# First feed-forward half step in two phases: products of half size upward, then downward in groups of four tiles

## The chip, the cores and the metric

The kernel runs on one core of one Trainium2 chip. The metric is the device time of one execution in microseconds (us), from several runs of each kernel. Engines are named as in the profile: PE is TensorE (matmuls; PEld its weight loads), DVE VectorE, ACT ScalarE, POOL GpSimd, and SP the queue that issues most transfers.

## The reference

One layer over 512 latent and 256 context tokens of width 1024: a SwiGLU half step on both streams, a two-part recurrent mixer, a second half step on the latent tokens, a last norm. All is float32. What the change touches is the first half step:

```python
def swiglu(h, w1, w2):
    g, u = jnp.split(h @ w1, 2, axis=-1)
    return (jax.nn.silu(g) * u) @ w2

def ffn_sub(s, mods, nw, w1, w2):
    shift, scale, gate = mods
    return s + 0.5 * gate * swiglu(modulate(rmsnorm(s, nw), shift, scale), w1, w2)

x = ffn_sub(x, mod_lat[0:3], norm1_w[l], ffn1_w1[l], ffn1_w2[l])          # 512 tokens
s_ctx = ffn_sub(s_ctx, mod_ctx[0:3], norm1_w[l], ffn1_w1[l], ffn1_w2[l])  # 256 tokens
...
x = x + mod_lat[5] * lat_mix
x = ffn_sub(x, mod_lat[6:9], norm3_w[l], ffn2_w1[l], ffn2_w2[l])
return rmsnorm(x, final_norm_w)
```

`w1` is 1024 x 5632 (gate and up halves of 2816 columns each), `w2` 2816 x 1024.

## The kernel before

Activations lie transposed: 128 rows of the width on the partitions, tokens along the free dimension, so that x is 8 tiles (index k or m) of 768 columns, 256 of the context first (`CTX`), then 512 latent ones (`LAT`). Each float32 matrix product is three matmuls on operands split into a high and a low part (`split`, line 78: ACT writes the high part, DVE the low part; `gemm3`, line 248: high x high, high x low, low x high).

The half step runs over 22 tile pairs j of 128 columns, a gate and an up tile each. For each pair, `up` (line 402) makes 8 x 3 matmuls of 512 columns and 8 x 3 of 256 for the gate tile, and as many for the up tile; `act` applies silu and the product and splits the result. After every two pairs, `down` (line 439) multiplies their results with `w2` for each of the 8 tiles of x: 6 matmuls of 512 columns and 6 of 256, and a DVE instruction that adds the PSUM bank times the gate to x. Up and down alternate in PE's program order. The last pair is computed by segments (`up_last`), and its down step runs over three segments of 256 columns while the next norm begins.

The second half step (latent tokens only) already computes most of its pairs another way (`up_fast`, line 306, `ups_fast`, line 375): the pair's 2 x 2 blocks (gate/up by token half, two halves of the width) come from seven block products of half the size (Winograd's form of Strassen's scheme), with sums of weight blocks (S1 to S4, on DVE) and of activation blocks (T1 to T4, made once by `fast_operands`). A product is 4 x 3 matmuls of 256 columns there. It works in steps that are woven between units: `b` is a PSUM bank that takes product after product, and ACT copies it out between them.

Beside this, `hook` (in `_build`, line 1037 on) computes the adaLN modulation for later stages: each of 56 tiles is a 512 KB load and one or two dot products on DVE (`mod_tile`, line 215). In the start phase `more` and its helpers prepare the norm of tile k while PE works on k-1.

Each engine runs its instructions in its own program order. Within `ordered` stretches that is the order written; elsewhere a scheduler fixes it at build time, and semaphores carry the waits. SP issues the loads in order too, and waits there for the buffer that a load fills.

Of the kernel before, what the change touches and what calls it, by code (L numbers as in the profile page):

```python
# [12 lines left out]
P = 128  # L13
# [55 lines left out]

class Builder:  # L70
# [12 lines left out]

    def sq_add(self, S, k, x, n, lanes="vpvpvpvl"):

        nc = self.nc
        lane = lanes[k]
        if n > 512:
            sq = self.fp.tile([P, n], F32, name="ah" if lane in S else "al", bufs=3)
# [125 lines left out]
    def mod_tile(self, i, k):  # L215
        nc = self.nc
        wm = self.modp.tile([P, DM], F32, name="wm", bufs=3)
# [39 lines left out]
    def ffn(self, w1, w2, with_ctx, gate_l, gate_c, hook, first, ahead, then, final=None, more=None, fast=None):  # L257
        nc = self.nc
        G = 2
        off = 0 if with_ctx else NC_  # L260
        AT = NT - off
        segs = [LAT, CTX] if with_ctx else [LAT]

        def load(j):
            ws, banks = self.ffn_load(w1, j)
            return ws, banks + ([self.ps.tile([P, 512], F32, name="mm")] if with_ctx else [])
# [8 lines left out]
        def mm(part, half, k, joint=False):  # L275
# [3 lines left out]
            if with_ctx:  # L279
                st, en = ((k == 0 and half == 0), (k == KT - 1 and half == 1)) if joint else (None, None)  # L280
                self.gemm3(pss[2][:, half * 256:half * 256 + 256], h, l, self.xh[k][:, :NC_], self.xl[k][:, :NC_],
                           k, KT, st, en)

        def act_tiles(j):
            return load2(j), [self.fp.tile([P, AT], dt, name=n, bufs=bufs)
                              for n, dt, bufs in (("sg", F32, 2), ("ah", F32R, 3), ("al", F32R, 3))]

        def gated(part, tiles, lo, n):

            psg, psu = part[1][:2]  # L290
            g, u = ((psg[:, lo - NC_:lo - NC_ + n], psu[:, lo - NC_:lo - NC_ + n]) if lo >= NC_ else
                    (part[1][2][:, :256], part[1][2][:, 256:]))
            sg = tiles[0][:, lo - off:lo - off + n]
            nc.scalar.activation(sg, g, AF.Silu)
            nc.vector.tensor_tensor(out=sg, in0=u, in1=sg, op=ALU.mult)

        def act(part, j):
            w2, tiles = act_tiles(j)
            for lo, n in segs:
                gated(part, tiles, lo, n)  # L300
            sg, ah, al = tiles
            self.split(ah, al, sg)
            self.split(*w2)
            return w2[0], w2[1], tiles[1], tiles[2]

        def up_fast(j):

            H = DM // 2
            half = lambda w: (w[:, :H], w[:, H:])
            pair = lambda: (self.wp.tile([P, DM], F32R, name="whi"), self.wp.tile([P, DM], F32R, name="wlo"))
            u, g = (self.wp.tile([P, DM], F32, name="wraw", bufs=2) for _ in range(2))
            for i, raw in ((0, g), (1, u)):
                nc.sync.dma_start(out=raw, in_=w1[j, i])
            s21, s34 = (fast["s"][:, 2 * (j % 2) + i, :] for i in range(2))
            (S2, S1), (S3, S4), (A11, A12), (A21, A22) = half(s21), half(s34), half(u), half(g)
            self.tt(S1, A21, A22, ALU.add)
            self.tt(S2, S1, A11, ALU.add)  # L320
            self.tt(S3, A11, A21, ALU.add)
            self.tt(S4, S2, A12, ALU.add)
            wa = pair()
            self.split(*wa, u)
            wd = [self.fp.tile([P, H], F32R, name="wd" + x, bufs=2) for x in "hl"]
            self.split(*wd, A22)
            yield
            ws = pair()
            self.split(*ws, s21)
            yield  # L330
            b, a = (self.ps.tile([P, 512], F32, name="mm")[:, :256] for _ in range(2))

            def product(bank, w, at, x, start, stop):
                for q in range(4):
                    ks = slice(at + q * P, at + (q + 1) * P)
                    xh, xl = x(q)
                    for i, (l, r) in enumerate(((w[0], xh), (w[0], xl), (w[1], xh))):
                        nc.tensor.matmul(bank, lhsT=l[:, ks], rhs=r, start=(start and q == 0 and i == 0),
                                         stop=(stop and q == 3 and i == 2), skip_group_check=True)

            block = lambda k0, seg: lambda q: tuple(t[k0 + q][:, seg[0]:seg[0] + seg[1]] for t in (self.xh, self.xl))
            T1, T2, T3, T4 = fast["t"]
            ev = self.fp.tile([P, 3, 256], F32, name="ev", bufs=2)
            p1, u2, u3 = (ev[:, i, :] for i in range(3))
            product(b, wa, 0, block(0, LAT_A), True, True)
            nc.scalar.copy(out=p1, in_=b)
            product(a, wa, H, block(4, LAT_A), True, True)
            self.tt(p1, a, p1, ALU.add)
            yield
            wr = pair()  # L350
            self.split(*wr, s34)
            yield
            product(b, ws, 0, T2, False, True)
            nc.scalar.copy(out=u2, in_=b)
            yield
            c = self.ps.tile([P, 512], F32, name="mm")[:, :256]
            product(c, ws, H, T1, True, True)
            yield
            product(b, wr, 0, T3, False, True)
            nc.scalar.copy(out=u3, in_=b)  # L360
            w2, (sg, ah, al) = act_tiles(j)
            self.tt(sg[:, 256:], c, u3, ALU.add)
            self.split(*w2)
            yield
            product(b, wd, 0, T4, False, True)
            nc.scalar.activation(sg[:, :256], b, AF.Silu, scale=-1.0)
            nc.scalar.activation(sg[:, 256:], sg[:, 256:], AF.Silu, scale=-1.0)
            product(c, wr, H, block(4, LAT_B), False, True)
            self.tt(u2, c, u2, ALU.add)
            both = sg.rearrange("p (h t) -> p h t", h=2)  # L370
            self.tt(both, ev[:, 0:2, :], both, ALU.mult)
            self.split(ah, al, sg)
            yield w2[0], w2[1], ah, al

        def ups_fast(js, turn, done):


            nxt, old = up_fast(js[0]), None
            next(nxt), next(nxt)
            for j in js:  # L380
                cur, nxt = nxt, up_fast(j + 1) if j != js[-1] else None
                next(cur)
                turn()
                if old:
                    done(next(old))
                next(cur)
                if nxt:
                    next(nxt)
                next(cur)
                turn()  # L390
                next(cur)
                if nxt:
                    next(nxt)
                turn()
                next(cur)
                turn()
                old = cur
            turn()
            turn()
            done(next(old))  # L400

        def up(j):
            part = load(j)
# [5 lines left out]
        def up_last(j):  # L409

            part = load(j)
            w2, tiles = act_tiles(j)
            self.split(*w2)
            banks = part[1]
            for lo, n in ((LAT, CTX) if with_ctx else (LAT_A, LAT_B)):
                self.mm_seg([(*part[0][half], banks[half] if lo >= NC_ else banks[2],
                              lo - NC_ if lo >= NC_ else half * 256) for half in range(2)], (lo, n))
                gated(part, tiles, lo, n)
                sg, ah, al = (t[:, lo - off:lo - off + n] for t in tiles)
                self.split(ah, al, sg)  # L420
            return w2[0], w2[1], tiles[1], tiles[2]

        def up_first(js):

            ps = []
            for q, ws in enumerate(first):
                bank = lambda pool, name: pool.tile([P, 512], F32, name=name)
                ps.append((ws, [bank(self.ps, "mm"), bank(self.ps, "mm"),
# [996 lines left out]
```

## Time and profile before

| | before |
|---|---|
| runs | 1355.25, 1349.97, 1352.85 us; median 1352.85 us |
| profiled execution | 1351.87 us, span 1350.1 us |
| busy in the span | PE 1326.4 us (98%), PEld 1183.7 (88%), DVE 943.2 (70%), ACT 512.1 (38%), POOL 39.6 (3%) |
| start, norm and first two pairs | 0 to 75 us |
| first half step, steady | 111 to 587 us |
| mixer and its output projection | about 612 to 1020 us |
| second half step | about 1020 us to the end |

The span is the time between the first and the last instruction of the profile; 1.77 us of the execution lie around it. "Busy" is a union of modelled durations, and matmuls overlap in the pipeline: a matmul of 512 columns is listed with 0.39 us although the next one starts 0.23 us later. What PE needs is therefore read from starts, not from durations.

### The profile page before, as it was taken

The numbers are of one execution on the slowest core, as the hardware profiler recorded it, in microseconds if no ns is written. First come the engines' busy times: TensorE is split into PE (matmuls) and PEld (weight loads), VectorE is DVE, ScalarE is ACT, GpSimd is POOL, SyncE is SP. The second block draws the span as 40 slices with busy tenths as digits, with TensorE's granted clock in tenths as the row PEclk, the third lists the DMA queues.
The fourth block names the chain that finished last, engine by engine and source line by source line (L and its number), as shares of the span: only waits on it lengthen the run. The fifth ranks groups of instructions, "written<-read, shape, count | busy, mean of one in ns | idle before, by whom it ended". The sixth has DMA issues, their size and how long they took to land.

```text
span 1350.1 us, 20599 instructions
## 1 busy us (share of the span) xinstructions
PE 1326.4 (98%) x8426; PEld 1183.7 (88%) x8426; DVE 943.2 (70%) x1540; ACT 512.1 (38%) x894; POOL 39.6 (3%) x51
## 2 busy tenths in 40 slices
PE   8999999999999999999989999999999999999997
PEld 4788888888888888899988788888998999999996
DVE  6988767645645644477497777896668878888765
ACT  5541112112112112176464443444554444444434
POOL 1100000000000000021100000000000000000001
PEclk8999999999999999999999999999999999999998
DMA  7654444234334321022132111113324322223301
GB/s 291 227 175 156 141 140 157 94 125 156 109 110 156 114 90 47 32 81 94 47 106 84 47 32 48 47 64 109 126 94 165 102 94 94 94 94 110 110 17 63
DMA packets 43235, 143.17 MB, mean 106 GB/s; under 512 B 4722, under 2 KB 9202, under 8 KB 43140
## 3 DMA queue, kind: packets, MB, share of 16 engines
q1 hardware_dynamic: 43140, 141.85, 31.2%
q8 instruction: 66, 1.08, 0.3%
q14 instruction: 29, 0.24, 0.1%
HBM read 137.60 MB, written 4.24 MB: 105 GB/s over the span
## 4 chain that ended last, share of the span: by engine, by line
PE 92%; DVE 4%; issue 2%; DMA 1%; ACT 1%; POOLq 0%; POOL 0%; DVEq 0%
PE mm L56 64%; PE aux L56 29%; DVE mod_scr L56 1%; DVE wlo L56 1%; DMA wraw<-in_wo 1%; ACT whi L56 0%; DMA wraw<-in_f1w 0%; DVE x L56 0%; DVE rms_acc L56 0%; DVE s L56 0%; DVE xl L56 0%; DVE w2lo L56 0%; DVE a L56 0%; ACT xh L56 0%; DMA w2lo<-in_cc 0%
## 5 line engine op out<-in xcount | busy, mean ns | idle before, releaser
L56 PE MATMUL mm<-xh,whi 128*128 128x256 f32 (+1 forms) x1460 | 477.4, 328 | 1.2 <-ACT xh L56 1.2
L56 PE MATMUL mm<-xh,wlo 128*128 128x256 f32 (+1 forms) x1460 | 472.8, 325 | 0.8 <-DVE wlo L56 0.8
L56 PE MATMUL mm<-xl,whi 128*128 128x512 f32 (+1 forms) x1392 | 457.1, 329 | 2.8 <-DVE xl L56 2.8
L56 PEld LDWEIGHTS mm<-xh,whi 128*128 128x128 f32 x1460 | 277.4, 190 | 28.1 <-issue 1.8
L56 PEld LDWEIGHTS mm<-xh,wlo 128*128 128x128 f32 x1460 | 276.8, 190 | 24.1 <-DVE wlo L56 1.0
L56 PEld LDWEIGHTS mm<-xl,whi 128*128 128x128 f32 x1392 | 264.7, 190 | 26.3 <-DVE xl L56 4.1
L56 ACT ACTIVATE whi<-wraw 128x1024 fp32r<-128x1024 f32 x100 | 105.6, 1059 | 184.4 <-issue 99.1
L56 DVE TENSOR_TENSOR wlo<-wraw,whi 128x1024 fp32r<-128x1024 f32 x100 | 121.8, 1221 | 73.4 <-ACT whi L56 73.3
L56 PE MATMUL aux<-ah,w2hi 128*128 128x512 f32 (+1 forms) x480 | 171.6, 358 | 0.1
L56 PE MATMUL aux<-al,w2hi 128*128 128x512 f32 (+1 forms) x480 | 170.7, 356 | 0.0
L56 PE MATMUL aux<-ah,w2lo 128*128 128x512 f32 (+1 forms) x480 | 169.9, 354 | 0.0
L56 DVE SCALAR_TENSOR_TENSOR x<-aux,mod_l,x 128x512 f32<-128x512 f32 x160 | 117.7, 746 | 27.7 <-PE aux L56 27.3
L56 DVE CUSTOM_DVE_ANT_0 mod_scr<-wm,cb 128x1024 bf16<-128x1024 f32 x96 | 118.8, 1238 | 9.1 <-DMA wm<-in_w_mod 7.3
L56 PEld LDWEIGHTS aux<-ah,w2lo 128*128 128x128 f32 x480 | 90.8, 189 | 12.9
L56 PEld LDWEIGHTS aux<-ah,w2hi 128*128 128x128 f32 x480 | 91.0, 190 | 11.7 <-ACT ah L56 0.6
L56 PEld LDWEIGHTS aux<-al,w2hi 128*128 128x128 f32 x480 | 91.1, 190 | 10.1
L56 ACT ACTIVATE w2hi<-w2raw 128x1024 fp32r<-128x1024 f32 x44 | 44.6, 1050 | 138.4 <-PE aux L56 135.3
L56 DVE TENSOR_TENSOR sg<-mm,sg 128x512 f32<-128x512 f32 (+1 forms) x49 | 27.2, 562 | 87.8 <-PE mm L56 69.9
L56 ACT ACTIVATE sg<-mm 128x256 f32<-128x256 f32 (+1 forms) x66 | 30.1, 458 | 132.4 <-PE mm L56 132.4
L56 PE MATMUL mm<-tl,whi 128*128 128x256 f32 x204 | 57.7, 283 | 0.0
L56 DVE TENSOR_TENSOR w2lo<-w2raw,w2hi 128x1024 fp32r<-128x1024 f32 x44 | 53.7, 1220 | 1.8 <-ACT w2hi L56 0.6
L56 DVE TENSOR_TENSOR wlo<-s,whi 128x1024 fp32r<-128x1024 f32 x34 | 41.6, 1224 | 17.7 <-ACT whi L56 17.7
(295 smaller groups left out, 1956.6 us busy)
## 6 DMA issues: line engine op xcount, KB each, us to landing
wm<-in_w_mod SPq DMA_DIRECT2D x64, 512.0 KB, 4.7
wraw<-in_f2w SPq DMA_DIRECT2D x44, 512.0 KB, 3.3
wraw<-in_f1w SPq DMA_DIRECT2D x42, 512.0 KB, 3.3
wraw<-in_wi SPq DMA_DIRECT2D x32, 512.0 KB, 3.3
w2raw<-in_f1w SPq DMA_DIRECT2D x24, 512.0 KB, 3.3
w2raw<-in_f2w SPq DMA_DIRECT2D x22, 512.0 KB, 4.3
wraw<-in_wo SPq DMA_DIRECT2D x8, 512.0 KB, 5.4
x<-in_xT SPq DMA_DIRECT2D x8, 384.0 KB, 4.9
```

Of the source, the lines that this page charges most:

```text
L56: r = f(*a, **kw)
```

## The change

The first half step becomes a function of its own, `ffn1`, in two phases. Its first four pairs stay as they were in the up direction (the first two in the start phase). The other 18 pairs (j = 4 to 21) are computed by seven products of half size, as in the second half step, on halves of 384 of the 768 columns: 7 x 12 matmuls of 384 columns. No down step runs between them. Each pair's result (128 x 768) is written to device memory by a POOL transfer (`keep`). Then the down phase runs over five groups of four pairs, and a last one of two: each group's results are loaded again and split, and for each of the 8 tiles of x there are 12 matmuls of 512 and 12 of 256 columns and one addition to x for each segment. `w2` is laid out anew, so that one load serves two tiles of x and four pairs. The modulation tiles are spread over both phases, one per unit and one per tile of x.

x is normalised in place in the start phase, its buffer serves as scratch in the up phase, and x is loaded a second time (POOL, 8 transfers) before the down phase. Buffers of the stage come from a class with three shared names (`six`, `four`, `two`). The second half step and the mixer keep their instruction order on PE, DVE and ACT; in the second half step one copy goes to another tile.

```diff
+class Space1:
+    def tile(self, shape, dt, name=None, bufs=None):
+        return self.pool.tile(shape, dt, name="six", bufs=8)
+    quad = lambda self, dt: self.pool.tile([P, DM], dt, name="four", bufs=5)
+    pair = lambda self: self.pool.tile([P, DM], F32R, name="two", bufs=2)
+    wide = lambda self: self.b.modp.tile([P, NT], F32, name="wm", bufs=2)
+    sums = lambda self, j: [self.quad(F32) for _ in range(2)]
...
+    def up_half(self, w1, j, W, c0, T, space):
+        for i, raw in ((0, g), (1, u)):
+            nc.sync.dma_start(out=raw, in_=w1[j, i])
+        s21, s34 = space.sums(j)
+        (S2, S1), (S3, S4), (A11, A12), (A21, A22) = half(s21), half(s34), half(u), half(g)
+        self.tt(S1, A21, A22, ALU.add)
...
+        wa = pair()
+        self.split(*wa, u)
+        wd = space.last()
+        self.split(*wd, A22)
+        yield
+        ws = pair()
+        self.split(*ws, s21)
+        yield
+        b, a = bank(), bank()
...
+        product(b, wa, 0, block(0, c0), True, True)
+        nc.scalar.copy(out=p1, in_=b)
+        product(a, wa, H, block(4, c0), True, True)
+        self.tt(p1, a, p1, ALU.add)
+        yield
+        wr = pair()
+        self.split(*wr, s34)
+        yield
+        product(b, ws, 0, T2, False, True)
+        nc.scalar.copy(out=u2, in_=b)
+        yield
+        c = bank()
+        product(c, ws, H, T1, True, True)
+        yield
+        product(b, wr, 0, T3, False, True)
...
+        nc.scalar.copy(out=g2, in_=b)
+        self.tt(g2, c, g2, ALU.add)
+        yield
+        product(b, wd, 0, T4, False, True)
+        nc.scalar.activation(g1, b, AF.Silu, scale=-1.0)
+        nc.scalar.activation(g2, g2, AF.Silu, scale=-1.0)
+        product(c, wr, H, block(4, c0 + W), False, True)
+        self.tt(u2, c, u2, ALU.add)
+        both = sg.rearrange("p (h t) -> p h t", h=2)
+        self.tt(both, up_, both, ALU.mult)
+        yield sg
...
+    def ffn1(self, space, first, more, hook, mods, ahead, then):
+        hs = [self.dram.tile([P, NT], F32, name=f"h{j}") for j in range(NJ)]
+        keep = lambda j, sg: nc.gpsimd.dma_start(out=hs[j], in_=sg)
...
+        ops = self.half_operands(space.x, 384, space.operands())
+        unit = lambda j: self.up_half(w1, j, 384, 0, space.T, space)
...
+        self.ups_half(range(4, NJ), unit, nxt, turn, keep)
+        for m in range(KT):
+            nc.gpsimd.dma_start(out=space.x[:, m, :], in_=T["xT"][m])
...
+        for g in range(5):
+            for m in range(KT):
+                if m % 2 == 0:
+                    load_w2(*((g, m // 2 + 1) if m < 6 else (g + 1, 0)))
+                wh, wl = w2[g, m // 2]
+                for seg, gate in ((LAT, self.mod_l), (CTX, self.mod_c)):
+                    lo, n = seg
+                    pb = bank(self.ps, "mm") if n > 256 else bank(self.aux, "aux")
+                    for k in range(4):
+                        ks = slice((m % 2 * 4 + k) * P, (m % 2 * 4 + k + 1) * P)
+                        ah, al = (t[:, lo:lo + n] for t in group[g][k])
+                        self.gemm3(pb[:, :n], wh[:, ks], wl[:, ks], ah, al, k, 4)
+                    x = self.seg_x(seg, m)
+                    self.stt(x, pb[:, :n], gate[:, 2, m:m + 1], x, ALU.mult, ALU.add)
+                if m in (2, 4) and (g < 4 or m == 2):
+                    load_h(g + 1, m // 2 - 1)
+                hook(NJ)
...
+        self.down_last(last, segs, then)
```

Three places show how the order of the engines changes. In the tile names, `mm` and `aux` are PSUM banks, `sg` a gate tile, `whi` and `wlo` the parts of a weight tile.

The first is ACT in the steady up work. Before, two tile pairs and the down step of the two before them take this:

```order
L56 ACTIVATE w2hi<-w2raw 128x1024 x2
L56 ACTIVATE sg<-mm 128x512
L56 ACTIVATE whi<-wraw 128x1024 x2
L56 ACTIVATE sg<-mm 128x256
L56 ACTIVATE ah<-sg 128x768
L56 ACTIVATE sg<-mm 128x512
L56 ACTIVATE whi<-wraw 128x1024 x2
L56 ACTIVATE sg<-mm 128x256
L56 ACTIVATE ah<-sg 128x768
```

Now one unit, with the numbers of the banks (`mm_1318` is this unit's bank b, `mm_1190` the one of the unit before; `four_1256` holds S3 and S4, `two` the pair's last weight block, `x_92` is the scratch in x):

```order
L56 COPY x_92<-mm_1318 128x384
L56 ACTIVATE whi_1375<-four_1256 128x1024
L56 ACTIVATE x_92<-mm_1190 128x384
L56 ACTIVATE two_1393<-wraw_1380 128x512
L56 ACTIVATE whi_1389<-wraw_1379 128x1024
L56 COPY x_92<-mm_1318 128x384
L56 ACTIVATE whi_1422<-four_1383 128x1024
L56 COPY x_92<-mm_1318 128x384
L56 ACTIVATE x_92<-x_92 128x384
```

Instead of four reads of banks for two pairs there are four for each unit, three of them copies between products on the same bank, and splits of weights stand between the first copy and the second.

The second place is DVE at the end of the start phase, where the low part `xl` of the last tile of x, k = 7, is made in two pieces (512 latent columns, 256 of the context). Before:

```order
L56 TENSOR_SCALAR s_159<-s_159,cst 128x2
L56 TENSOR_TENSOR lb<-lbl,lb_mx 128x8
L56 TENSOR_SCALAR oml<-lb 128x8
L56 TENSOR_TENSOR xl<-nm_y,xh 128x512
L56 TENSOR_TENSOR xl<-nm_x,xh 128x256
L56 TENSOR_TENSOR sg<-mm,sg 128x512
L56 TENSOR_TENSOR sg<-mm,sg 128x256
L56 TENSOR_TENSOR wlo<-wraw,whi 128x1024 x2
```

Now:

```order
L56 TENSOR_SCALAR s_155<-s_155,cst 128x2
L56 TENSOR_TENSOR xl<-x,xh 128x512
L56 TENSOR_TENSOR x<-x 128x4x384
L56 TENSOR_TENSOR xl<-x,xh 128x256
L56 TENSOR_TENSOR six<-wraw,six 128x1024
L56 TENSOR_TENSOR x<-x 128x4x384
L56 TENSOR_TENSOR wlo<-wraw,whi 128x1024
L56 TENSOR_TENSOR six<-mm,six 128x512
```

A sum of activation blocks (`128x4x384`, 1536 columns) stands between the two pieces; another one of that size (T1) stands further ahead, between the two dot products of k = 5.

The third place is DVE in the down work. Before, once the results of two pairs are there:

```order
L56 SCALAR_TENSOR_TENSOR x<-aux,mod_l,x 128x512 x6
L56 SCALAR_TENSOR_TENSOR x<-aux,mod_c,x 128x256 x8
L56 TENSOR_TENSOR w2lo<-w2raw,w2hi 128x1024
L56 ISA mod_scr,mod_l<-wm,cb 128x1024
L56 ISA mod_l 128x1
```

Now, in the first group of four:

```order
L56 SCALAR_TENSOR_TENSOR x<-mm,mod_l,x 128x512
L56 SCALAR_TENSOR_TENSOR x<-aux,mod_c,x 128x256
L56 ISA mod_scr,mod_l<-wm,cb 128x1024
L56 ISA mod_l 128x1
L56 TENSOR_TENSOR wlo<-wraw,whi 128x1024
L56 ISA mod_scr,mod_c<-wm,cb 128x1024
L56 ISA mod_c 128x1
L56 SCALAR_TENSOR_TENSOR x<-mm,mod_l,x 128x512
L56 SCALAR_TENSOR_TENSOR x<-aux,mod_c,x 128x256
```

The additions to x now come in couples, half as many in all, and two dot products of a modulation tile stand between one couple and the next.

## Rows read from the trace of the kernel before

**Rows 1.** The profile's page, part 1: busy time of each engine.

```profile
PE 1326.4 (98%) x8426; PEld 1183.7 (88%) x8426; DVE 943.2 (70%) x1540; ACT 512.1 (38%) x894; POOL 39.6 (3%) x51
```

**Rows 2.** Chain of waits, first half step: start, length (us), engine, tile, count.

```profile
193.06 16.66 PE aux L56 x96
209.72 33.60 PE mm L56 x192
```

**Rows 3.** Windows: busy time (count) of PE, PEld, DVE, ACT, POOL; PEclk; DMA.

```profile
60.00:84.00 24.00, 24.00 (x139) 20.87 (x138) 17.74 (x32) 16.54 (x24) 0.00 (x0) 1.00 0.35 113
160.00:210.00 50.00, 50.00 (x288) 43.97 (x287) 34.66 (x54) 9.20 (x13) 0.00 (x0) 1.00 0.39 127
1100.00:1310.00 210.00, 209.99 (x1433) 194.69 (x1432) 166.61 (x233) 93.06 (x144) 0.00 (x0) 1.00 0.28 93
```

**Rows 4.** Chain of waits, second half step: one product of 256 columns.

```profile
1110.37 1.43 PE mm L56 x12
```

**Rows 5.** Timeline of PE in a down step: start, length, instruction.

```profile
203.35 0.39 PE L56 MATMUL aux<-al,w2hi 128*128 128x512 f32 x1
203.58 0.39 PE L56 MATMUL aux<-ah,w2lo 128*128 128x512 f32 x1
203.81 0.28 PE L56 MATMUL aux<-ah,w2hi 128*128 128x256 f32 x1
203.92 0.28 PE L56 MATMUL aux<-al,w2hi 128*128 128x256 f32 x1
```

**Rows 6.** DVE groups by shape, 110 to 590 us: busy, mean ns | idle.

```profile
L56 DVE CUSTOM_DVE_ANT_0 mod_scr<-wm,cb 128x1024 bf16<-128x1024 f32 x64 | 78.2, 1222 | 8.6 <-DMA wm<-in_w_mod 7.3
L56 DVE SCALAR_TENSOR_TENSOR x<-aux,mod_l,x 128x512 f32<-128x512 f32 x80 | 58.8, 748 | 23.1 <-PE aux L56 22.7
L56 DVE TENSOR_TENSOR wlo<-wraw,whi 128x1024 fp32r<-128x1024 f32 x36 | 44.1, 1225 | 61.5 <-ACT whi L56 61.5
L56 DVE SCALAR_TENSOR_TENSOR x<-aux,mod_c,x 128x256 f32<-128x256 f32 x80 | 38.7, 484 | 16.5 <-PE aux L56 16.5
...
L56 DVE TENSOR_TENSOR al<-sg,ah 128x768 fp32r<-128x768 f32 x18 | 17.1, 952 | 5.5 <-ACT ah L56 5.5
L56 DVE TENSOR_TENSOR sg<-mm,sg 128x512 f32<-128x512 f32 x19 | 13.1, 691 | 75.1 <-PE mm L56 66.0 <-ACT sg L56 9.1
L56 DVE TENSOR_TENSOR sg<-mm,sg 128x256 f32<-128x256 f32 x19 | 7.9, 418 | 0.0
```

**Rows 7.** ACT groups by shape in the second half step, 1110 to 1290 us.

```profile
L56 ACT ACTIVATE whi<-s 128x1024 fp32r<-128x1024 f32 x23 | 24.4, 1061 | 27.2 <-PE mm L56 27.2
L56 ACT COPY ev<-mm 128x256 f32<-128x256 f32 x35 | 12.9, 369 | 38.2 <-PE mm L56 38.1
...
L56 ACT ACTIVATE wdh<-wraw 128x512 fp32r<-128x512 f32 x11 | 6.9, 624 | 9.9 <-PE mm L56 9.9
L56 ACT ACTIVATE sg<-sg 128x256 f32<-128x256 f32 x12 | 5.0, 419 | 14.8 <-DVE sg L56 14.8
```

**Rows 8.** The page, part 6: transfers, KB each, median us from issue to landing.

```profile
wm<-in_w_mod SPq DMA_DIRECT2D x64, 512.0 KB, 4.7
wraw<-in_f1w SPq DMA_DIRECT2D x42, 512.0 KB, 3.3
```

**Rows 9.** Timeline of DVE at the end of the start phase.

```profile
68.51 0.69 DVE L56 TENSOR_TENSOR xl<-nm_y,xh 128x512 fp32r<-128x512 f32 x1 [1.31 <-ACT nm_y L56]
69.50 0.43 DVE L56 TENSOR_TENSOR xl<-nm_x,xh 128x256 fp32r<-128x256 f32 x1 [0.29 <-ACT nm_x L56]
```

**Rows 10.** Timeline of PE at the same place: the context part of k = 7, and pair 2.

```profile
71.85 0.28 PE L56 MATMUL mm<-xl,whi 128*128 128x256 f32 x1
...
75.24 0.40 PE L56 MATMUL mm<-xh,whi 128*128 128x512 f32 x1
```

**Rows 11.** Timeline of POOL and DVE in the start phase, 26 to 31 us.

```profile
26.98 2.45 POOL L56 TENSOR_TENSOR ah<-x,sg 128x768 f32<-128x768 f32 x1 [7.81 <-ACT sg L56]
...
27.68 2.83 DVE L56 CUSTOM_DVE_ANT_0 mod_scr<-wm,cb 128x1024 bf16<-128x1024 f32 x1
```

More of the change, by code (lines that the diff above doesn't have):

```diff
@@ L88, in sq_add @@
         if n > 512:
[L89 removed]
+            sq = self.tmp.tile([P, n], F32)
         elif lane in S:
@@ new lines, in ups_half @@
+    def ups_half(self, js, unit, nxt, turn, done):
+        old = None
+        for j in js:
+            cur, nxt = nxt, unit(j + 1) if j != js[-1] else None
+            next(cur)
+            turn(j, 0)
+            if old:
+                done(j - 1, next(old))
+            next(cur)
+            if nxt:
+                next(nxt)
+            next(cur)
+            turn(j, 1)
+            next(cur)
+            if nxt:
+                next(nxt)
+            turn(j, 2)
+            next(cur)
+            turn(j, 3)
+            old = cur
+        turn(j, 4)
+        done(j, next(old))
@@ new lines, in down @@
+    def down(self, parts, seg, m0, width, pool, gate, S=None, final=None, off=0):
+        nc = self.nc
+        lo, w = seg
+        banks = [pool.tile([P, 512], F32, name="aux" if pool is self.aux else "mm") for _ in range(width)]
+        for q, (h, l, ah, al) in enumerate(parts):
+            for m in range(m0, m0 + width):
+                ms = slice(m * P, (m + 1) * P)
+                self.gemm3(banks[m - m0][:, :w], h[:, ms], l[:, ms], ah[:, lo - off:lo - off + w],
+                           al[:, lo - off:lo - off + w], q, len(parts))
+        for m in range(m0, m0 + width):
+            x = self.seg_x(seg, m)
+            self.stt(x, banks[m - m0][:, :w], gate[:, m:m + 1], x, ALU.mult, ALU.add)
+            if S is not None:
+                self.todo_add()
+                self.todo_add = self.sq_add(S, m, x, w)
+                if final is not None:
+                    nc.scalar.activation(x, x, AF.Copy, scale=final[:, m:m + 1])
+                else:
+                    self.todo_add()
+                    self.todo_add = lambda: None
@@ L258, in ffn, with ffn2 @@
+    def ffn2(self, w1, w2, gate, first, then, final, fast):
         nc = self.nc
         G = 2
[L260 to L266, printed above, removed]
         def load2(j):
@@ L273, in load2, with mm @@
             return w2h, w2l, w2r
-        def mm(part, half, k, joint=False):
+        def mm(part, half, k):
             ws, pss = part
@@ L288, in gated @@
[L288 to L293, printed above, removed]
+        class Space:
+            sums = lambda _, j: (fast["s"][:, 2 * (j % 2) + i, :] for i in range(2))
+            last = lambda _: [self.fp.tile([P, DM // 2], F32R, name="wd" + x, bufs=2) for x in "hl"]
+            up = lambda _, j: self.fp.tile([P, 2, 256], F32, name="ev", bufs=2)
+            gate = lambda _, j: self.fp.tile([P, NL], F32, name="sg", bufs=2)
@@ L294, in gated, with act_tiles @@
+        space = Space()
+        def act_tiles():
+            return [self.fp.tile([P, NL], F32R, name=n, bufs=3) for n in ("ah", "al")]
+        def gated(part, sg, lo, n):
+            g, u = (p[:, lo - NC_:lo - NC_ + n] for p in part[1])
+            sg = sg[:, lo - NC_:lo - NC_ + n]
             nc.scalar.activation(sg, g, AF.Silu)
-            nc.vector.tensor_tensor(out=sg, in0=u, in1=sg, op=ALU.mult)
+            self.tt(sg, u, sg, ALU.mult)
         def act(part, j):
-            w2, tiles = act_tiles(j)
@@ L299, in act @@
-            for lo, n in segs:
-                gated(part, tiles, lo, n)
-            sg, ah, al = tiles
+            w2, sg, (ah, al) = load2(j), space.gate(j), act_tiles()
+            gated(part, sg, *LAT)
             self.split(ah, al, sg)
             self.split(*w2)
[L304 to L400, printed above, removed]
+            return w2[0], w2[1], ah, al
@@ L402, in up @@
         def up(j):
-            part = load(j)
+            part = self.ffn_load(w1, j)
             for half in range(2):
@@ L409, in up_last @@
         def up_last(j):
-            part = load(j)
-            w2, tiles = act_tiles(j)
+            part = self.ffn_load(w1, j)
+            w2, sg, tiles = load2(j), space.gate(j), act_tiles()
             self.split(*w2)
[L414 to L428, printed above, removed]
-                                bank(self.aux, "aux") if q else bank(self.ps, "mm")]))
-            for k in range(KT):
-                ahead_ = more(k)
-                for p in ps:
-                    for half in range(2):
-                        mm(p, half, k, joint=True)
-                        next(ahead_, lambda: None)()
-            self.ordered = True
-            return [act(p, j) for p, j in zip(ps, js)]
@@ L461, in ffn @@
-        start = up_first((0, 1)) if with_ctx else [act(p, j) for j, p in enumerate(first)]
-        parts, turns = [], []
-        hook(0)
-        self.ordered = False
-        hook(1)
+            for lo, n in (LAT_A, LAT_B):
+                self.mm_seg([(*part[0][half], part[1][half], lo - NC_) for half in range(2)], (lo, n))
+                gated(part, sg, lo, n)
+                self.split(*(t[:, lo - NC_:lo - NC_ + n] for t in (*tiles, sg)))
+            return w2[0], w2[1], *tiles
+        parts, turns, late = [], [], {}
@@ L1307, in then @@
                 return self.seg_norm(seg, 3, b) + ([spill] if lo >= NC_ else [])
-            self.ffn(T["f1w1"], T["f1w2"], True, self.mod_l[:, 2, :], self.mod_c[:, 2, :], hook, first, ahead, then,
-                     more=more)
+            self.ffn1(space, first, more, hook, mods, ahead, then)
             start = self.mixer_start(box["ws"])
```

303 lines of the change are left out of this document (202 added, 101 removed).

## The prediction

> **What bounds the kernel now.** I read the page's busy times first: PE is busy 98% of the span, DVE 70%, ACT 38% [rows 1]. That alone doesn't say that PE sets the time, so the chain of waits comes next. In the first half step it names nothing but PE: 33.60 us of up work for two tile pairs, 16.66 us of down work for two, and so on without a gap from 111 to 561 us; one period of each stands in [rows 2]. The windows say the same: 50.00 us of PE in 50, at a granted clock of 1.00, which is the upper level of 2.4 GHz, with DVE at 34.66 us [rows 3]. The reader is to see that no wait ends late there: every matmul taken away shortens the span, as long as nobody else becomes late. The second half step, which already uses the seven products on 256 columns, is as full: 209.99 of 210 us [rows 3].
>
> **The price of a matmul.** Durations in the timeline overlap, so I take starts. In the down step 512 columns go every 0.23 us and 256 columns every 0.11 to 0.12 us [rows 5]. The sums are sharper. A couple of one 512 and one 256 takes 33.60 / 96 = 0.350 us in the up work [rows 2], and 256 columns take 1.43 / 12 = 0.119 us in the second half step [rows 4], which leaves 0.231 us for 512. No row shows 384 columns. The ends are these two: 0.119 and 0.231 us. I take 0.175, half the couple, since 384 lies in the middle and nothing in the rows suggests a step between the two.
>
> **What the change removes and adds on PE.** For 18 pairs the up work falls from 48 couples each (8 tiles of x, gate and up, three matmuls) to 84 matmuls of 384 columns. Before: 18 x 48 x 0.350 = 302.4 us. After: 18 x 84 x 0.175 = 264.6 us. The gain is 37.8 us; at the ends of the price it would be 122 us (180 us after) or a loss of 47 us (349 us after). The down work keeps its matmuls, in another order: 16.66 us for two pairs, as now.
>
> The Trainium skill weighs a matmul otherwise: "TensorE: Matmul & The Clock Gate", section "Wait — 56ns, not 53.3ns?", puts the start-to-start time at columns over 2.4 GHz plus a fixed 2.5 ns. The rows lie 12 to 18 ns above columns over 2.4 GHz, so the measurement decides for the price. By the page 82,944 columns and 216 matmuls less would give 34.6 + 0.5 = 35 us, an estimate, 3 us short of mine.
>
> **DVE in the up phase.** A unit has three low parts of 1024 columns (3 x 1.225), one of 512 and four weight sums of 512 (5 x 0.69), three additions from a bank of 384 (0.55, between 0.691 and 0.418), a product of 768 (0.95) and two dot products (2 x 1.22) [rows 6]: 3.68 + 3.45 + 1.65 + 0.95 + 2.44 = 12.2 us, in a unit of 84 x 0.175 = 14.7 us. That is 83%; the second half step runs at 166.61 / 210 = 79% and loses nothing [rows 3]. I charge nothing; the cover is the 2.5 us that DVE is idle in each unit.
>
> **ACT in the up phase, the tight place.** Bank b takes four products one after the other, and ACT has to copy it out between them. In the second half step down work stands between; here nothing does. I lay a unit out in pieces of 2.1 us: b (0 to 2.1), a (to 4.2), the last two products of the unit before (to 8.4), T2 on b (to 10.5), T1 on c (to 12.6), T3 on b. T3 waits for the copy of T2. By the order of ACT, ahead of that copy stand the high part for wr (it waits for the last product of the unit before, at 8.4), a silu, a high part of 512 and one of 1024: 8.4 + 1.06 + 0.42 + 0.62 + 1.06 = 11.6 us [rows 7]. The copy of 384 (0.37 at 256 columns, so about 0.43) ends at 12.0, 0.6 us before T3. The low part for wr is through by about 10.7 us. The two high parts wait for weight loads of 3.3 us [rows 8], whose buffers come free, in the same layout, about 3.4 and 0.7 us before the unit begins; even 9 us for a load would do. So PE should go on without a wait, with 0.6 us to spare. That is my choice; the other end is the slower rival below.
>
> **The start.** The scheduler puts two sums of activation blocks before DVE is done with the norm. Each has 1536 columns: 1.24 ns a column (0.95 / 768) makes 1.9 us. At k = 7 the context part of xl is ready at 69.93 us and needed at 71.85 [rows 9, 10], a margin of 1.9 us. The first sum shifts the whole chain by 1.9; the second stands between the two pieces and costs 1.9 less the 0.3 us that DVE idles there now. So PE waits some 1.6 us there. Normalising in place makes ACT's second pass wait for its first, a few tenths at k = 0. The earlier loads (buffers are more plentiful) help nothing that waits now: DVE is full. I charge 1.8 us, and take -1 and 5 as the ends. The other sums and splits of T1 to T4 take about 14 us of DVE beside pairs 2 and 3 (33.6 us of PE), where the dot products of a dozen modulation tiles stood before; I charge nothing.
>
> **The down phase.** For one tile of x PE needs 12 x 0.350 = 4.2 us. DVE needs 0.75 + 0.48 for the additions, 2.44 for two dot products and half a low part, 0.61: 4.28 us in the first group [rows 6], so it falls behind by under 1 us in a group; five banks for 512 columns and three for 256 cover 8 us. From the second group on there is one dot product: 3.1 us, and 0.5 for the reloaded results. The results are written 15 us and more before they are loaded, and loaded a group ahead. The first group begins with the splits of pairs 0 to 3, for which the last three products of the up phase leave 8 us. I charge 0.8 us for the joint, from 0 to 6.
>
> **Sum.** The profiled execution took 1351.87 us, 1350.1 of them span. 1351.87 - 37.8 + 1.8 + 0.8 = 1316.7 us; the median of the runs is 1.0 above the profiled one, so 1317.5 us. The mixer and the second half step stay as they are. A difference under 0.5% (6.8 us) cannot be told from none here.
>
> **Rivals.**
> Part of the gain goes back. If ACT or DVE is later than worked out, T3 waits in each of 17 units: 0.5 to 1.5 us each gives 9 to 26 us, so 1326 to 1343. For it: 0.6 us is little, and DVE queues strictly behind transfers. Against it: the second half step shows no such loss at the same shares. Chance 0.16.
>
> POOL's transfers come late. POOL issues none now, and where it works on tiles DVE is hit: a dot product of 1.22 us takes 2.83 while POOL runs [rows 6, 11]. The result of pair 2 must be stored before a constant (`lvm`) can be loaded into its buffer, DVE waits for that constant ahead of the splits of units 4 and 5, and SP's queue stands behind it. Pair 2 ends near 95 us, its store and the loads of two constants take about 3 x 4.7 us [rows 8], so DVE goes on near 110; it must come to wr's low part by about 120 (unit 4 begins near 112, its T3 8.4 us later). That leaves some 9 us; a store 16 us late would cost 7 us once, so 1325. Chance 0.04.
> A page of the Trainium skill makes this a trap: "SBUF — State Buffer", section "SBUF: two separate sides", says that a transfer issued by POOL has its descriptors written by POOL, and starves while DVE holds the port that they share. The row on POOL and DVE agrees that the two stand in each other's way; that it holds up a transfer is shown by no run here.
>
> No difference: the wait at T3 comes to 1.7 to 2.5 us in each unit and eats the gain. Chance 0.03.
>
> Slower: the same wait over 2.5 us. Its place is T3 on bank b behind ACT's queue, its price 17 us for each us of wait, and it decides from 2.1 us on (35.2 / 17, par) and by over 0.5% from 2.5 us on. ACT would have to be 3 us late in every unit, for instance by a weight load that lands 3 us after ACT comes to its split; then 1351.87 + 0.98 - 35.2 + 17 x 3 = 1369 us. Or a matmul of 384 columns costs like one of 512: 37.8 gained becomes 47 lost, 1402 us. Against both: rows 2 to 4 show a price that goes with the columns, and loads of 3.3 us. Chance 0.05 for the two.
>
> Faster than worked out: a price of 384 columns under the middle, 0.165 us, would give 15 us more, 1302. Chance 0.04.
>
> **How the numbers follow.** The forecast has 0.68 and its own range is 1311 to 1325, its charges at their bounds. The range of 8 in 10 takes most of the case "part goes back" and some of the lower price: 1309 to 1332. Faster by over 0.5%: 0.68 + 0.16 + 0.04 + 0.04 = 0.92; the same 0.03; slower 0.05.
>
> **What will show it.** The groups by shape list 1512 matmuls of 384 columns, and twelve of them take 2.1 us in the chain. Windows in the up phase show PE full, DVE near 83%. The up phase of 18 units takes 265 us, each down group 33.6. In the start PE has a gap of 1 to 2 us at k = 7. I am wrong if PE waits for ACT's copies unit after unit, if twelve matmuls take over 2.2 us, or if DVE in the first down group holds a bank.

## The result and the profile after

The changed kernel takes 1312.88 us (median of 4 runs, 1311.93 to 1314.27), the kernel before 1351.51 us (4 runs, 1349.97 to 1355.25): a ratio of 0.9711, 95% interval 0.9687 to 0.9735. The profiled execution took 1313.55 us, 1311.7 of them span, which is 38.3 us less than the profiled one of before. The prediction was 1317.5 us with a range of 1309 to 1332.

The page of the changed kernel, part 1 (busy time of each engine), answers to [rows 1]:

```profile
PE 1285.8 (98%) x8210; PEld 1179.6 (90%) x8210; DVE 1007.8 (77%) x1612; ACT 575.2 (44%) x987; POOL 56.3 (4%) x81
```

PE is as full as before, with 216 matmuls fewer; DVE, ACT and POOL do more. Its chain of waits (start, length in us, engine, tile, count) answers to [rows 2]:

```profile
78.97 298.68 PE mm L56 x1716
377.65 1.42 PE aux L56 x12
379.07 2.75 PE mm L56 x12
...
575.83 53.57 PE mm L56 x394
...
1273.61 16.81 PE mm L56 x138
```

The whole up phase is one piece of PE; in the down phase the 512-column and 256-column banks of a tile of x alternate, 4.18 us for both. The starts of four matmuls on PE's timeline cut the first half step into its parts (before: pair 2 at 75.24 [rows 10]):

```profile
23.64 0.51 PE L56 MATMUL mm<-xh,whi 128*128 128x512 f32 x1 [1.20 <-ACT xh L56]
...
112.55 0.34 PE L56 MATMUL mm<-xh,whi 128*128 128x384 f32 x1
...
375.64 0.39 PE L56 MATMUL mm<-six,whi 128*128 128x512 f32 x1
...
541.93 3.28 PE L56 MATMUL mm<-six,four 128*128 128x256 f32 x26
```

The 18 units last from 112.55 to 375.64, 263.09 us, and the five groups of four downs to 541.93, 166.3 us. The window over the units says what the engines did in it (busy and count of PE, PEld, DVE, ACT, POOL; granted clock; DMA):

```profile
112.55:375.64 263.09, 263.09 (x1519) 262.77 (x1518) 202.53 (x285) 111.51 (x165) 12.95 (x24) 1.00 0.46 154
```

PE is never idle, DVE is busy 77% and ACT 42% of it. Of the kernel before, PE's timeline has three more rows that are needed below: the first matmul of the start, its one wait between 30 us and pair 2, and the first matmul of the last two pairs' down work:

```profile
23.59 0.49 PE L56 MATMUL mm<-xh,whi 128*128 128x512 f32 x1 [1.20 <-ACT xh L56]
...
38.86 0.50 PE L56 MATMUL mm<-xl,whi 128*128 128x512 f32 x1 [1.31 <-DVE xl L56]
...
578.04 0.28 PE L56 MATMUL mm<-ah,w2hi 128*128 128x256 f32 x1
```

And its chain has two that answer to the last two above:

```profile
611.90 53.57 PE mm L56 x394
...
1311.19 16.81 PE mm L56 x138
```

By the same places the 38.3 us come together as follows (us, minus is a gain).

| part | forecast | measured | how |
|---|---|---|---|
| first matmul to pair 2 | +1.8 | +3.5 | 55.17 (23.64 to 78.81) against 51.65 |
| pairs 2 and 3 | 0 | +0.1 | 33.74 against 33.60 |
| 18 units | -37.8 | -39.3 | 263.1 against 302.4 |
| down groups | +0.8 | -0.3 | 166.3 against 10 x 16.66 |
| rest, same instructions | 0 | -2.3 | 575.83 to 1273.61 is 697.8, 611.90 to 1311.19 is 699.3; the tail 0.8 less |

The last line is scatter: the stretch between its two marks holds the same instructions in every kernel run here, and lasted 697.3 to 699.8 us in them. What is to be explained is the start, which lost twice what was charged, and whether the units' gain is the matmuls' alone.

**The start.** The two engines beside each other in the changed kernel, POOL and DVE from 27 to 36 us:

```profile
27.32 7.95 POOL L56 TENSOR_TENSOR x<-x 128x768 f32<-128x768 f32 x3 [8.03 <-ACT x L56]
...
28.01 2.83 DVE L56 CUSTOM_DVE_ANT_0 mod_scr<-wm,cb 128x1024 bf16<-128x1024 f32 x1
30.77 0.08 DVE L56 DVE_READ_ACCUMULATOR2_ANT a<- 128x1 f32 x1
30.88 2.73 DVE L56 CUSTOM_DVE_ANT_0 mod_scr<-wm,cb 128x1024 bf16<-128x1024 f32 x1
33.55 0.08 DVE L56 DVE_READ_ACCUMULATOR2_ANT a<- 128x1 f32 x1
33.66 1.64 DVE L56 TENSOR_SCALAR a<-a,b,cst 128x2 f32<-128x2 f32 x1
```

POOL multiplies parts 2, 4 and 6 of x by the roots, and before, only the first of these stood here [rows 11]; each later one waited for a buffer until the norm was done with an earlier part. In place, in one tile for all of x, nothing holds them, and the three run one behind the other. Three DVE instructions in a row then take 2.83, 2.73 and 1.64 us, where the same forms take 1.22, 1.22 and 0.29 later on. Behind them PE waits three times, 3.06 us in all, where before it waited once, 1.31 us (38.86, above):

```profile
37.35 0.50 PE L56 MATMUL mm<-xh,two 128*128 128x512 f32 x1 [1.24 <-DVE two L56]
...
39.24 0.22 PE L56 MATMUL aux<-ident,row 2*128 2x2 f32 x1 [1.03 <-ACT row L56]
...
40.68 0.51 PE L56 MATMUL mm<-xl,whi 128*128 128x512 f32 x1 [0.79 <-DVE xl L56]
```

And the clock falls, as the windows say (columns as above):

```profile
35.00:41.00 6.00, 2.94 (x14) 1.65 (x12) 5.93 (x11) 3.94 (x8) 0.27 (x1) 1.00 0.46 171
41.00:45.00 4.00, 4.00 (x21) 2.54 (x19) 3.93 (x7) 1.90 (x3) 0.00 (x0) 0.57 0.98 358
```

PE was busy 2.94 of 6 us, and in the 4 us after that it was granted 0.57 in the mean, most of them at the lower of its levels, 1.2 GHz. That is the second part of the start's loss, and two of the runs below give its size. With ordinary pairs, and with five VectorE instructions held in each unit, PE waits at the same three matmuls and the third wait ends as far behind the first matmul (17.1 us, here 17.0), but the clock stays at 1.00 from 41 to 45 us, and pair 2 begins 53.71 and 53.61 us behind the first matmul. So about 2.0 of the 3.5 us go with the waits and 1.5 with the clock. Why the clock fell in one kernel and not in the others is not shown.

### The profile page after: what moved, and what is told of

Read it like the earlier page. It is cut to its first block, busy times and chain, and to the rows that moved or that the text cites. A ratio compares the mean times of both kernels' runs of the same rounds, so it can differ in the third digit from the quotient of the medians.

```text
span 1311.7 us, 20549 instructions
## 1 busy us (share of the span) xinstructions
PE 1285.8 (98%) x8210; PEld 1179.6 (90%) x8210; DVE 1007.8 (77%) x1612; ACT 575.2 (44%) x987; POOL 56.3 (4%) x81
## 4 chain that ended last, share of the span: by engine, by line
PE 93%; DVE 3%; ACT 2%; issue 1%; DMA 0%; POOL 0%; SPq 0%; POOLq 0%; DVEq 0%
PE mm L56 72%; PE aux L56 21%; DVE mod_scr L56 1%; DMA x<-in_xT 0%; ACT xh L56 0%; DVE x L56 0%; ACT six L56 0%; ACT nm_y L56 0%; DVE wlo L56 0%; DVE xl L56 0%; ACT whi L56 0%; DVE rms_acc L56 0%; POOL rms_acc L56 0%; DVE s L56 0%; DVE nm_x L56 0%
## 5 line engine op out<-in xcount | busy, mean ns | idle before, releaser
L56 PE MATMUL mm<-xh,whi 128*128 128x256 f32 (+2 forms) x1084 | 349.1, 323 | 1.2 <-ACT xh L56 1.2
L56 PE MATMUL mm<-xh,wlo 128*128 128x256 f32 (+2 forms) x1084 | 345.8, 320 | 0.8 <-DVE wlo L56 0.8
L56 PE MATMUL mm<-xl,whi 128*128 128x256 f32 (+2 forms) x1016 | 327.9, 323 | 2.9 <-DVE xl L56 2.9
L56 PEld LDWEIGHTS mm<-xh,whi 128*128 128x128 f32 x1084 | 205.6, 190 | 14.5 <-ACT xh L56 1.9
L56 PEld LDWEIGHTS mm<-xh,wlo 128*128 128x128 f32 x1084 | 205.6, 190 | 10.7 <-DVE wlo L56 1.0
L56 PE MATMUL mm<-six,whi 128*128 128x384 f32 (+1 forms) x752 | 209.2, 359 | 0.0
L56 PEld LDWEIGHTS mm<-xl,whi 128*128 128x128 f32 x1016 | 192.9, 190 | 14.7 <-DVE xl L56 4.4
L56 PEld LDWEIGHTS mm<-six,whi 128*128 128x128 f32 x752 | 135.5, 188 | 10.0
L56 PE MATMUL mm<-six,wlo 128*128 128x384 f32 (+1 forms) x376 | 134.4, 357 | 0.0
L56 PEld LDWEIGHTS mm<-six,wlo 128*128 128x128 f32 x376 | 70.6, 188 | 6.5
```

The lines of the kernel that those rows point to most:

```text
L56: r = f(*a, **kw)
```

## The experiments

Two theories are tested: the units gain what the matmuls' columns give, and the start loses by POOL's three products. Beside them stand the margins on which the prediction relied.

**Undoing the seven products.** Two phases, stores and groups of four stay; pairs 4 to 21 go the way of pairs 2 and 3, and the sums and splits of activation blocks are not made.

```
-  for j in (2, 3): (ordinary pair)
-  self.ups_half(range(4, NJ), unit, nxt, turn, keep)
+  for j in range(2, NJ): (ordinary pair, hook(j) at its half)
```

> Two phases, the store and the groups of four stay, but all 22 pairs of tiles are multiplied in the ordinary way (48 matmuls of 512 and 256 columns a pair), and the four operands are not made. Theory (the gain is the columns of the seven products, and the two phases give nothing): the 18 pairs take 302.4 us again in place of 263.1, so 39.3 us above the changed kernel, 1350 to 1355 us, ratio to the kernel before 0.999 to 1.003, and the start late by the same 3.6 us. Rival (a part of the gain comes from downs in groups of four and from the modulation dots being moved): 1340 us or less, ratio 0.992 or less.

Measured: 1355.13 us, ratio 1.0025 (1.0014 to 1.0037). The chain, with the up phase and the first piece behind the downs, then a window of the start:

```profile
78.94 338.86 PE mm L56 x1932
...
582.26 7.20 PE mm L56 x60
```

```profile
41.00:45.00 4.00, 3.21 (x22) 2.18 (x22) 3.93 (x9) 2.98 (x5) 0.00 (x0) 1.00 1.01 372
```

In the changed kernel the piece that answers to the second row begins at 542.09, 40.2 us earlier. So the seven products bring all of the gain, 42 us between the two medians, and the two phases by themselves bring none: between the medians they cost 3.8 us. In the profile the start has only 2.1 of them (53.71 us against 51.65, not the 3.6 that were expected), since the clock did not fall. The first matmul came 1.5 us later (25.07), and no run shows whether that belongs to the kernel.

**One pair more.** Pair 3 becomes a unit, 19 of 22.

```
-  for j in (2, 3):
+  for j in (2,):   ...   nxt = unit(3); self.ups_half(range(3, NJ), ...)
```

> The seven products for one pair more (19 of 22; pair 3 joins). Theory (time goes by the matmuls alone, 84 x 0.174 = 14.6 us in place of 16.8 us a pair): 2.2 us less than the changed kernel, 1310.7 us, ratio to the kernel before 0.9695. Rival (VectorE cannot make four operands and the next pair's weights, some 15 us of work, beside one pair of 16.8 us, and TensorE waits at the second half-size sum): 1313 to 1318 us, with gaps on TensorE between 95 and 105 us.

Measured: 1311.70 us, ratio 0.9708 (0.9695 to 0.9721).

```profile
79.36 296.45 PE mm L56 x1704
...
540.25 7.20 PE mm L56 x60
```

From pair 2 to the second row PE needs 460.89 us, against 463.12 (78.97 to 542.09) in the changed kernel: 2.2 us less, as expected, and no wait. Between the medians it is 1.2 us, which the scatter of the runs doesn't separate from 2.2. DVE's 15 us beside one pair were hidden.

**POOL's products to VectorE.**

```
-ROOT_P = (2, 4, 6)
+ROOT_P = ()
```

> The changed kernel, but the three products of x with the row of roots for parts 2, 4 and 6, which GpSimd does one behind the other from 27.3 to 35.3 us, are given to VectorE (3 x 0.95 us). Theory (VectorE's 2.83, 2.73 and 1.64 us beside them are GpSimd's doing, 4.5 us more than the same instructions take alone, and put the start 3.6 us late): the second dot takes 1.2 us and the third instruction 0.3, the first matmul of pair 2 comes at 75 to 77 us in place of 78.8, and the time is 1310 to 1311.5 us. Rival (the start is late because VectorE has the two half-operand sums of 1.75 us more to do): with 2.85 us more work on VectorE the start gets later, 80 to 82 us, and the time 1314 to 1316 us.

Measured: 1311.03 us, ratio 0.9701 (0.9688 to 0.9714). DVE at the same place:

```profile
27.97 1.22 DVE L56 CUSTOM_DVE_ANT_0 mod_scr<-wm,cb 128x1024 bf16<-128x1024 f32 x1
29.11 0.08 DVE L56 DVE_READ_ACCUMULATOR2_ANT a<- 128x1 f32 x1
29.23 1.22 DVE L56 CUSTOM_DVE_ANT_0 mod_scr<-wm,cb 128x1024 bf16<-128x1024 f32 x1
30.38 0.08 DVE L56 DVE_READ_ACCUMULATOR2_ANT a<- 128x1 f32 x1
30.50 0.29 DVE L56 TENSOR_SCALAR a<-a,b,cst 128x2 f32<-128x2 f32 x1
```

The three are short again, the clock stays at 1.00 from 35 to 45 us, and pair 2 begins at 74.81, 51.2 us behind the first matmul in place of 55.2: with more work on DVE the start is 4 us shorter, which excludes the rival. The profiled time is 2.8 us lower, since the identical rest was 1.2 us longer in this profile; the median is 1.9 us lower. The cleared start also shows the wait that the prediction had placed at k = 7. DVE, then PE:

```profile
68.59 0.69 DVE L56 TENSOR_TENSOR xl<-x,xh 128x512 fp32r<-128x512 f32 x1 [1.74 <-ACT x L56]
69.20 1.75 DVE L56 TENSOR_TENSOR x<-x 128x1536 f32<-128x1536 f32 x1
70.87 0.42 DVE L56 TENSOR_TENSOR xl<-x,xh 128x256 fp32r<-128x256 f32 x1
...
71.34 0.39 PE L56 MATMUL mm<-xl,whi 128*128 128x256 f32 x1 [0.84 <-DVE xl L56]
```

A sum of 1.75 us stands between the two low parts, and PE waits 0.84 us. In the changed kernel it stands there too (73.18 to 74.85), but PE comes late itself and waits under 0.1.

**Both edits.**

> Both edits together: 19 of 22 pairs by seven products and the three products of the start on VectorE. If both theories hold, the gains add: 4 to 5 us less than the changed kernel, 1308 to 1309 us. If one of them fails, the better of the two alone.

Measured: 1308.83 us, ratio 0.9683 (0.9670 to 0.9696). That is 4.1 us under the changed kernel, as expected if both add; by the medians the two alone gave 1.2 and 1.9.

**Both, and the sums behind the low part.**

```
+  with self.tc.issue_after(self.last_xl.ins):
       self.tt(t3, b22, b12, ALU.subtract); self.tt(t2, b22, t1, ALU.add)
```

> 19 of 22 pairs by seven products, the three products of the start on VectorE, and the second and third half-operand sums put behind the low part of x's last part. In the run with the first two edits one such sum (1.75 us) lay between the two low parts of the last part of x, and TensorE waited 0.7 to 1.0 us for the second of them. Theory (that sum made the wait): the wait goes, and the time is 0.7 to 1.0 us below that run, 1307.8 us. Rival (the sums are needed early: the next pair's second product waits for an operand that comes later): 1309 to 1312 us, with a wait at 95 to 100 us.

Measured: 1308.52 us, ratio 0.9676 (0.9662 to 0.9689). The wait at k = 7 is gone, and the start from first matmul to pair 2 takes 50.2 us, 1.0 less than with both edits. Between the medians that is 0.3, within their scatter. This is the fastest kernel of the case, 4.4 us under the changed one.

**The same edit in the kernel before.**

> The kernel before, with its three products of the start for parts 2, 4 and 6 given from GpSimd to VectorE. There the three lie apart (26.98, 35.65, 46.09 us), and each stretches one VectorE instruction beside it (2.83 in place of 1.22, 1.66 and 1.80 in place of 0.29). Theory (4.5 us of stretch go, 2.85 us of work come, and of TensorE's one wait for it, 1.6 us at 37 us, the most part goes): 1 to 2 us less, ratio to the kernel before 0.9985 to 0.9992. Rival (spread over the start, they cost nothing that TensorE sees): 1.000, or up to 1.001 by the work added.

Measured: 1349.30 us, ratio 0.9982 (0.9973 to 0.9991), and 50.2 us from first matmul to pair 2 against 51.65. So POOL's products cost the start something before too, 1.4 us in that stretch, against 4.0 (55.2 to 51.2) in the changed kernel. Without them the changed kernel's start is still 1.0 longer than that of before (51.2 against 50.2), and the run with the sums behind the low part (50.2) shows that this is the sum at k = 7. The 3.5 us of the table are these two parts, 2.6 and 1.0, rounded.

**ScalarE's margin.** Copies of the finished bank are added ahead of the copy that T3 waits for.

```
+  for _ in range(3):           # 6 in the second run
+      nc.scalar.copy(out=space.x[:, KT, :W], in_=b)
   nc.scalar.copy(out=u2, in_=b)
```

> The changed kernel with three more copies of the finished bank on ScalarE (3 x 0.48 = 1.44 us) in each of the 18 units, between the last matmul of the second half-size sum and the copy that the third sum's first matmul waits for. In the trace of the changed kernel that copy ends 1.4 us ahead of the matmul. Theory by that row: no wait or under 0.1 us a unit, 1313 to 1315 us. Rival by the prediction's figure of 0.6 us of margin: TensorE waits 0.84 us a unit, 15 us, 1328 us.

Measured: 1317.52 us, between the two expectations. In the changed kernel ACT's copy and T3's first matmul (251.92) stand so:

```profile
250.03 0.48 ACT L56 COPY x<-mm 128x384 f32<-128x384 f32 x1 [1.19 <-PE mm L56]
...
251.92 0.51 PE L56 MATMUL mm<-six,whi 128*128 128x384 f32 x2
```

Here the four copies take 1.88 us, and a unit 14.81 us (T3 begins at 239.22 and at 254.03) in place of 14.56 (251.92 and 266.48): 0.25 us of wait, some 4 us in all. So the margin is near 1.2 us, twice the prediction's 0.6. The first high part in ACT's queue runs 4.2 us into the unit, not 8.4, so ACT is idle when T2 ends.

> Six more copies (2.88 us a unit) at the same place. Theory (1.4 us of margin): TensorE waits 1.5 us a unit, 27 us in all, 1339 us. Rival by 0.6 us of margin: 2.3 us a unit, 41 us, 1354 us. If ScalarE's work is hidden as the busy share (43%) would have it: 1313 us.

Measured: 1323.81 us, and only 0.3 us of wait in a unit. The order of PE was not the same: with more work ahead of the copy the scheduler put thirteen matmuls of another bank in front of T3. The run tells the price of the work as the scheduler can hide it, not that of the wait. (Of the 10.9 us some 4 lie ahead of the first matmul and in the identical rest.)

The same six copies, with every matmul of a unit held behind the one before it:

```
+  self.ordered = W == 384
   nc.tensor.matmul(...)
```

> The six extra copies of ScalarE in each unit again, now with the order of TensorE's matmuls held as in the changed kernel, so that nothing is put ahead of the third sum's product. Theory (1.2 to 1.4 us of margin, after it every us is waited for): 1.5 to 1.7 us a unit, 27 to 30 us in all, 1340 to 1343 us. Rival (what was measured without that hold is the whole price): 0.33 us a unit, 1319 to 1324 us.

Measured: 1365.97 us, ratio 1.0101 (1.0083 to 1.0120): 53 us over the changed kernel, more than the theory. ACT, then PE in one unit:

```profile
257.35 2.52 ACT L56 COPY x<-mm 128x384 f32<-128x384 f32 x5 [1.25 <-PE mm L56]
259.77 1.06 ACT L56 ACTIVATE whi<-four 128x1024 fp32r<-128x1024 f32 x1
260.73 0.85 ACT L56 COPY x<-mm 128x384 f32<-128x384 f32 x2
...
259.00 0.34 PE L56 MATMUL mm<-six,wlo 128*128 128x384 f32 x1
261.63 0.61 PE L56 MATMUL mm<-six,whi 128*128 128x384 f32 x2 [2.29 <-ACT x L56]
```

And the window behind that wait:

```profile
263.00:266.50 3.50, 3.50 (x13) 3.50 (x12) 3.29 (x8) 1.00 (x2) 0.00 (x0) 0.52 0.11 15
```

A high part of 1.06 us got between the copies, so PE is late by 2.46 us beyond its pace; 18 x 2.46 = 44 us. The window shows what some of the units lose besides: behind the wait the granted clock is 0.52 for 3.5 us. Five of the 18 lose it so and last 18.7 us; the others, with the same wait, last 17.1. The prediction's slower rival, a wait of some 2.5 us at T3, is a real mechanism, at a higher price than its 17 us for each us of wait, which give 42. The changed kernel is 1.2 us of ACT's work away from where the wait begins.

**VectorE's margin.** Three and five more instructions of 128x768 in a unit.

```
+  for _ in range(3):           # 5 in the second run
+      self.tt(r, r, r, ALU.max)     # r: the row of roots
```

> The changed kernel with three more 128x768 instructions on VectorE (3 x 0.95 = 2.85 us) in each of the 18 units. VectorE is busy 11.3 of the 14.6 us of a unit. Theory (only a full engine bounds, and the order has room): 14.1 of 14.6 us, no change, 1313 to 1316 us. Rival (VectorE's work lies on a chain with TensorE, so that work put ahead of a weight's low part makes TensorE wait before VectorE is full): 10 us or more slower, 1323 us or more.

> Five more of them (4.75 us a unit): VectorE would need 16.0 us a unit against TensorE's 14.6. Theory: VectorE becomes the bound of the 18 units, 1.4 us a unit, 26 us in all, 1339 us.

Measured: 1319.06 and 1319.02 us. Neither expectation fits: the loss is the same for both doses, and not in the units. The window of the second run over nine units:

```profile
118.00:250.00 132.00, 132.00 (x763) 131.92 (x763) 131.93 (x187) 55.25 (x82) 4.86 (x9) 1.00 0.39 135
```

DVE is full and PE still waits for nothing, because the added work, which nobody reads, was put where DVE had time. Some of it went into the start, ahead of the low parts at k = 7. PE waits there for DVE, as its timeline of the first run shows, and the clock falls behind the wait, as the window shows:

```profile
78.35 0.50 PE L56 MATMUL mm<-xl,whi 128*128 128x512 f32 x1 [1.11 <-DVE xl L56]
...
80.36 0.39 PE L56 MATMUL mm<-xl,whi 128*128 128x256 f32 x1 [1.16 <-DVE xl L56]
```

```profile
82.00:84.00 2.00, 2.00 (x8) 1.71 (x8) 2.00 (x2) 1.99 (x4) 0.00 (x0) 0.50 0.74 256
```

From first matmul to pair 2 (85.39 and 85.05) both take 59.8 us in place of 55.2, which is 4.6 of the 6.2 us lost. The first matmul itself came 2.0 and 1.6 us later in these profiles; what that depends on is not shown.

Held in their units:

```
+  self.ordered = True
   self.tt(r, r, r, ALU.max)
```

> The five extra VectorE instructions (4.75 us a unit), now each held behind the instruction before it, so that they stay in their unit and none gets into the start. Theory: VectorE needs 16.0 us of a unit against TensorE's 14.6 and becomes the bound: 1.4 us a unit, 26 us in all, 1339 us. Rival (back to back they take less than 0.95 us, and VectorE just fits): 1313 to 1318 us.

Measured: 1325.77 us, ratio 0.9804: 12.9 us, 0.7 a unit, between the two. DVE was busy 257.4 of the 265 us from 118 to 383. Where instructions follow each other they take some 0.87 us, not 0.95, and so part of the dose fitted. An estimate from this run (five times 0.87 less the 0.7 lost) puts the edge, from which DVE bounds, at some 3.6 us of added work in a unit; 14.6 less the 11.3 that DVE is busy give 3.3.

## Why the prediction was right

**The price of a matmul: right, and it carries the result.** 263.09 / 1512 = 0.1740 us against 0.175. The groups by shape of the changed kernel hold the 1512 as foretold (432, four times 216, and 216 of the product whose weights, both parts, lie in `two`):

```profile
L56 PE MATMUL mm<-six,whi 128*128 128x384 f32 x432 | 109.5, 334 | 0.0
L56 PE MATMUL mm<-xh,whi 128*128 128x384 f32 x216 | 72.1, 334 | 0.0
...
L56 PE MATMUL mm<-six,two 128*128 128x384 f32 x216 | 40.4, 334 | 0.0
```

The mean of 334 ns is a matmul's own length, which overlaps the next; the price is the pitch. The Trainium skill, "TensorE: Matmul & The Clock Gate", section "Wait — 56ns, not 53.3ns?", would have 384 / 2.4 + 2.5 = 162.5 ns, an estimate. The row says 174.0, and the row decides.

**DVE and ACT hidden: right, with more room than worked out.** 77% in place of 83%, and the doses put the edges at 3.3 to 3.6 us (DVE, an estimate) and 1.2 us (ACT) a unit. The tight place was named rightly and mis-sized by half, because the buffer for ACT's first high part comes free when the second product is through, not two products later.

**The joint and the down phase: right that it is small, and it is nothing.** The charge of 0.8 was not needed; no PE gap of 0.1 us stands between 375 and 541 us.

**The start: this step failed, though its size stayed inside its ends (-1 to 5).** It said that "the earlier loads (buffers are more plentiful) help nothing that waits now", and charged 1.8 us at k = 7. Measured are 3.5 us, and the waits stand at k = 1 to 3. Freeing the buffers let POOL run ahead, and what that does to DVE stood in [rows 11], which was read for POOL's transfers alone; the fall of the clock behind the waits, 1.5 us, had no term at all. The wait at k = 7 was rightly seen but is hidden behind the others here; once the start is cleared, PE waits 0.84 us there, and taking the sum away gives 1.0 us in place of the 1.8 charged. The Trainium skill, "SBUF — State Buffer", section "SBUF: two separate sides", calls the port pair that the two engines share an exclusive lock, held for a whole instruction; the stretched DVE rows, and their shortening when POOL's products went, agree with it.

**The rivals.** No part of the gain goes back in the units. POOL's transfers are not late: the stores land in 3.0 us in the median beside a DVE at 77%, and the constant of which the prediction feared a delay was cast at 111.53 us, against the 120 at which it would have counted (the page's part 6, and DVE's timeline):

```profile
h<-x POOLq DMA_DIRECT2D x18, 384.0 KB, 3.0
```

```profile
111.53 0.63 DVE L56 CAST lvm<-wm 128x896 uint8<-128x896 f32 x1 [0.44 <-DMA wm<-in_lvm]
```

The trap that the same section of the skill describes for such transfers is not seen here. The profiled time came out 3.2 us under the 1316.7 of the sum: the price gave 1.5, the down groups 1.1, the scatter of the untouched rest 2.3, and the start took 1.7 back. That the start's extra loss did not show in the total is luck: the scatter of the rest covered it. The other 1.5 us of the medians is how these stand to the profiled runs. Two sums of the prediction are off: 1316.7 and 1.0 are 1317.7, not 1317.5, and its charges at their bounds (start -1 to 5, joint 0 to 6) give 1314 to 1326, not 1311 to 1325.

## What to carry to other kernels

Where one engine fills a stretch, count its instructions and price them by the pitch of rows on either side; here that was right within 0.6%. When an edit frees buffers, ask which engine they held back: its work may now come all at once and stand in the way of another engine, as POOL's did in DVE's. A dose of work added to an engine measures a margin only if it is held in its place, since a scheduler that sees it will move it, or something else.

## What was not expected of the hardware

- A DVE instruction on 128x2 elements took 1.64 us beside POOL's product of 128x768, and 0.29 alone; giving POOL's three products (7.95 us there) to DVE (0.95 each) made DVE's chain shorter, by some 4 us in the start.
- A wait of PE can cost more than its length: 3 us of idling in 6 were followed by 4 us at a granted clock of 0.57, and a wait of 2.3 us by 3.5 us at 0.52 in five of 18 units. It need not: the other 13 units, and the start of two other runs with waits at the same matmuls, kept 1.00.
- VectorE at 131.93 of 132 us cost PE no wait at all.
